# Rotating mixer A's queries before their norm, with the norm's factor in the softmax

## The chip, the cores and the metric

One core of a Trainium2 chip runs the whole kernel. The metric is the time of one execution on the device in microseconds (us), the median over several runs. The engines are TensorE (PE in the profile, with PEld for its weight loads), VectorE (DVE), ScalarE (ACT), GpSimd (POOL) and SyncE (SP, which issues most transfers).

## The reference, cut to what matters

The layer normalises its input, projects it once (`w_in`), runs two mixers over head groups beside each other, gates their outputs, projects once more (`w_out`), normalises and adds the input. 16 meta tokens stand ahead of 512 real ones, so keys count 528 and the queries whose output is kept 512. Mixer A, which the change touches, has 8 query heads of 128 columns and 2 key/value heads:

```python
def rmsnorm(x, g):
    r = lax.rsqrt(jnp.mean(xf * xf, axis=-1, keepdims=True) + NORM_EPS)
    return (xf * r * g).astype(x.dtype)
def gqa_axial_mixer(qa, ka, va, q_g, k_g, ang_row, ang_col, pos):
    q = axial_rope(rmsnorm(heads_first(qa, A_HEADS, HEAD_DIM), q_g), ang_row, ang_col)
    k = axial_rope(rmsnorm(heads_first(ka, A_KV_HEADS, HEAD_DIM), k_g), ang_row, ang_col)
    ...
        s = jnp.einsum('bkgqd,bksd->bkgqs', qs[0], k).astype(jnp.float32) * scale
        p = jax.nn.softmax(s, axis=-1)
        return jnp.einsum('bkgqs,bksd->bkgqd', p.astype(v.dtype), v)
```

`r` is one number for a token and a head. `q_g` has one gain for each of the 128 columns. `axial_rope` rotates columns 0 to 31 with 32 to 63 by the row angle, and 64 to 95 with 96 to 127 by the column angle; the real tokens alone are rotated by nonzero angles.

## The kernel before, in words

All matrix products run on pairs of rounded numbers, a high part and a low part (`xh`, `xl`; `wh`, `wl`; `qh`, `qlA`), three matmuls for one product. Weights come from DRAM in pieces of 512 KB into `st` (three buffers); `wsplit` makes the high part on ScalarE (line 154) and the low part on VectorE (line 155).

**Order of work.** TensorE's order is written by the kernel itself. Class `Lanes` keeps a clock of estimated matmul time. A piece of attention work is a generator that issues some matmuls and yields a lag; `lanes.poll()`, called between the matmuls of a projection, resumes the generators that are due. So the transposes, scores and products of the heads are strewn into the projections, and each matmul is pinned behind the one before it. The other engines' orders come from a planner that walks through the whole program by its own estimates. When an engine is free it takes, among the instructions that are ready, the one with the earliest place in the program. `tc.high_priority(n)` moves that place forward by n positions, and a negative n moves it back. `wsplit` runs 60 positions late (`AHEAD`). Each engine then works through its queue strictly in that order.

**Mixer A.** `keys_A` makes the two key heads, normed and rotated, and is done when the queries begin. `queries_A(g)` projects four query heads at once (g is 0, then 1): four accumulators `pd`, one for each 128 tokens, each of 4 heads x 128 columns. ScalarE scales them by the token's input norm into `qn` (line 650). The generator `turn` then takes one of the four tiles at a time: `head_norm` (lines 570 to 580) squares each head on ScalarE with a row sum, makes the factor with `rstd` (two small GpSimd instructions, lines 239 and 241), and scales each head by factor and gain on VectorE (line 578); `rope` (lines 582 to 593) makes the swapped half products on VectorE into `t2` (lines 588 and 590), multiplies by the cosines on GpSimd (line 592) and adds on VectorE (line 593).

`attention_A`, one generator per head, transposes the four tiles of its head (line 66, `tr<-ident,qn`), splits the result into `qh` and `qlA`, and for each of four tiles of 128 queries: six score matmuls into `sc` (one buffer of two banks), the row maximum on VectorE (`mxA`, line 546), its scaling by -1/sqrt(128) on GpSimd (line 547), the exponential on ScalarE with row sums (line 550), the reciprocal, and the scaling of the probabilities on GpSimd (line 553). After two tiles `p_times_v` transposes the probabilities (`tr`, two buffers shared with all transposes and `pv`), splits them (`ph`, line 306; `pl`, line 309), multiplies by the values into `pv`, and VectorE multiplies that with the head's gate (`gA`, line 558).

Around this, TensorE projects: queries of group 0, gates 0 and 1 of mixer A, queries of group 1, gates 2 to 7, then the output projection. The heads of group 0 run beside the second of these and the third, those of group 1 beside the gates and the start of the output projection. The first head of group 1 (h = 4) begins its transposes only when `turn` of group 1 has issued all its work.

Of the kernel before, what the change touches and what calls it, by code (L numbers as in the profile page):

```python
# [10 lines left out]
F32 = mybir.dt.float32  # L11
# [6 lines left out]
P = 128  # L18
# [90 lines left out]
def kernel(ctx: ExitStack, tc: tile.TileContext, xT, xn, xm, w_s, w_t, w_q, w_o,  # L109
# [127 lines left out]
    def rstd(dst, ss, n, rows=P):  # L237

        nc.gpsimd.tensor_scalar(out=dst, in0=ss, scalar1=1.0 / n, scalar2=EPS,
                                op0=ALU.mult, op1=ALU.add)  # L240
        nc.gpsimd.tensor_tensor(out=dst, in0=dst, in1=mhalf[:rows, :dst.shape[1]], op=ALU.pow)  # L241
# [188 lines left out]
    def two(t):  # L430
        return t.rearrange("p (a b) -> p a b", a=2)
# [86 lines left out]
    def attention_A(h, qn, q_task, k, k_task, v, v_task):  # L518
        while h == 4 and not q_task[3]:
            yield 0.3  # L520
        gs = lambda half: gA[h][:, half * 256:(half + 1) * 256]
        qh = ap.tile([P, SEQ], F32R, name="qh", tag="q1")
        ql = ap.tile([P, SEQ], F32R, name="qlA", tag="q2")
        tr = ptr.tile([P, 512], F32, name="tr", tag="tr")
        for t in range(TT):
            transpose(tr[:, t * P:(t + 1) * P], qn[t][:, h % 4, :], ident)
        hi(qh, tr)
        lo(ql, tr, qh)
        yield LAG["qA"]
        while not k_task[3]:  # L530
            yield 0.3
        kh, kl = k
        last = None
        for half in range(2):
            pts = []
            for t in (2 * half, 2 * half + 1):
                tq = slice(t * P, (t + 1) * P)
                mx = ap.tile([P, 1], F32, name="mxA", tag="mx", bufs=4)
                sm = ap.tile([P, 1], F32, name="smA", tag="sm", bufs=4)
                yield from room(1)  # L540
                sc = psc.tile([P, 2, 512], F32, name="sc", tag="sc")
                for i, (n0, n1) in enumerate(KEYS):
                    mm(sc[:, i, :HALF], qh[:, tq], kh[:, n0:n1], start=True, stop=False)
                    mm(sc[:, i, :HALF], qh[:, tq], kl[:, n0:n1], start=False, stop=False)
                    mm(sc[:, i, :HALF], ql[:, tq], kh[:, n0:n1], start=False, stop=True)
                nc.vector.tensor_reduce(out=mx, in_=sc[:, :, :HALF], op=ALU.max, axis=AX.XY)
                nc.gpsimd.tensor_scalar(out=mx, in0=mx, scalar1=-ASCALE, scalar2=1.0,
                                        op0=ALU.mult, op1=ALU.mult)
                p = ap.tile([P, NT], F32, name="p", tag="p", bufs=6)
                nc.scalar.activation(two(p), sc[:, :, :HALF], AF.Exp, scale=ASCALE, bias=mx,  # L550
                                     accum_out=sm)
                nc.vector.reciprocal(out=sm, in_=sm)
                nc.gpsimd.tensor_scalar(out=p, in0=p, scalar1=sm, scalar2=1.0,
                                        op0=ALU.mult, op1=ALU.mult)
                pts.append(p)
                if t % 2 == 0:
                    yield LAG["scA"]
            last = spawn_pv(v_task, p_times_v(pts, v, lambda pv, half=half: nc.vector.tensor_tensor(  # L558
                out=gs(half), in0=pv, in1=gs(half), op=ALU.mult), h), LAG["pA"])
            if half == 0:  # L560
                yield LAG["scA"]
        over[NH + h] = lanes.spawn(spill_A(h), 0.0, last)
# [7 lines left out]
    def head_norm(raw, n, g, rows=P):  # L570

        ss = ap.tile([P, 4], F32, name="ssh", tag="ssh", bufs=4)
        for i in range(n):
            jk = ap.tile([P, P], F32, name="jk", tag="jk")
            nc.scalar.activation(jk[:rows], raw[:, i, :], AF.Square, accum_out=ss[:rows, i:i + 1])
        rstd(ss[:rows, :n], ss[:rows, :n], P, rows)
        for i in range(n):
            nc.vector.scalar_tensor_tensor(out=raw[:, i, :], in0=raw[:, i, :],  # L578
                                           scalar=ss[:rows, i:i + 1], in1=g[:rows], op0=ALU.mult,
                                           op1=ALU.mult)  # L580

    def rope(x, cos, sin):

        t2f = ap.tile([P, NT], F32, name="t2", tag="tT")
        t2 = t2f[:, :4 * P].rearrange("p (n a r) -> p n a r", n=4, a=2)
        xv = x.rearrange("p n (a r) -> p n a r", a=2)
        sv = sin.rearrange("p n (a r) -> p n a r", a=2)
        nc.vector.tensor_tensor(out=t2[:, :, :, 0:32], in0=xv[:, :, :, 32:64],
                                in1=sv[:, :, :, 0:32], op=ALU.mult)
        nc.vector.tensor_tensor(out=t2[:, :, :, 32:64], in0=xv[:, :, :, 0:32],  # L590
                                in1=sv[:, :, :, 32:64], op=ALU.mult)
        nc.gpsimd.tensor_tensor(out=x, in0=x, in1=cos, op=ALU.mult)  # L592
        nc.vector.tensor_tensor(out=x, in0=x, in1=t2f[:, :4 * P].rearrange(
            "p (n d) -> p n d", n=4), op=ALU.add)

    def keys_A(pss):
# [33 lines left out]

        return (kh, kl), lanes.spawn(turn(), LAG["vals"])

    def queries_A(g):

        pss = [pd.tile([P, 512], F32, name="pd", tag="pd") for _ in range(TT)]
        for k0 in range(0, KT, 2):
            wh, wl = fetch()
            for k in (k0, k0 + 1):
                c = slice((k - k0) * 512, (k - k0 + 1) * 512)
                for t in range(TT):  # L640
                    ts_ = slice(NM + t * P, NM + (t + 1) * P)
                    mm(pss[t], xh[k][:, ts_], wh[:, c], start=(k == 0), stop=False)
                    mm(pss[t], xl[k][:, ts_], wh[:, c], start=False, stop=False)
                    mm(pss[t], xh[k][:, ts_], wl[:, c], start=False, stop=(k == KT - 1))
                    lanes.poll()
        res = []
        for t in range(TT):
            tag = "ql" if g == 0 else "fr" if t < 2 else "f"
            qn = ap.tile([P, 4, P], F32, name="qn", tag=tag, bufs=2 if tag == "fr" else 4)
            nc.scalar.activation(qn.rearrange("p n d -> p (n d)"), pss[t], AF.Copy,  # L650
                                 scale=rt[:, t:t + 1])
            res.append(qn)

        def turn():
            for t, qn in enumerate(res):
                head_norm(qn, 4, gqB)
                rope(qn, cosT[:, t:t + 1, :].broadcast_to([P, 4, P]),
                     sinT[:, t:t + 1, :].broadcast_to([P, 4, P]))
                yield LAG["norm"]

        return res, lanes.spawn(turn(), 0.0)


    for h in range(NH):
# [374 lines left out]
```

## Time and profile before

| what | value |
|---|---|
| median of 3 runs | 955.04 us (954.67 to 955.67) |
| the profiled execution, its own time | 955.66 us |
| its span in the profile | 953.9 us |
| TensorE busy | 926.4 us, 97% of the span |
| VectorE busy | 584.6 us, 61% |
| ScalarE busy | 482.0 us, 51% |
| GpSimd busy | 164.0 us, 17% |
| mean granted TensorE clock | 0.99 of full speed |

The span is what the profiler saw of one execution, from its first to its last event; the execution's own time is a little longer. Times inside the profile count from the start of the span. The busy time of TensorE counts matmuls from start to modelled end, so that back-to-back matmuls show as 100%. An arrow in a row (`<-`) says what ended the idle time ahead of an instruction.

### The profile page before, as it was taken

The numbers are of one execution on the slowest core, as the hardware profiler recorded it, in microseconds if no ns is written. First come the engines' busy times: TensorE is split into PE (matmuls) and PEld (weight loads), VectorE is DVE, ScalarE is ACT, GpSimd is POOL, SyncE is SP. The second block draws the span as 40 slices with busy tenths as digits, with TensorE's granted clock in tenths as the row PEclk, the third lists the DMA queues.
The fourth block names the chain that finished last, engine by engine and source line by source line (L and its number), as shares of the span: only waits on it lengthen the run. The fifth ranks groups of instructions, "written<-read, shape, count | busy, mean of one in ns | idle before, by whom it ended". The sixth has DMA issues, their size and how long they took to land.

```text
span 953.9 us, 14190 instructions
## 1 busy us (share of the span) xinstructions
PE 926.4 (97%) x5498; PEld 810.8 (85%) x5498; DVE 584.6 (61%) x974; ACT 482.0 (51%) x845; POOL 164.0 (17%) x250
## 2 busy tenths in 40 slices
PE   9999999999999999999999999998999999999983
PEld 8899898989989898998997888886888888888862
DVE  6386576757575574757554274447554662476996
ACT  6664655546464554746552254354555743245531
POOL 0001010101001010101201041226212123201054
PEclk9999999999999999999999999999999999999996
DMA  9742122222223222312223223211222346976785
GB/s 333 260 159 99 67 88 88 79 77 100 76 78 99 82 84 77 100 67 78 89 67 100 89 68 109 67 58 54 80 75 78 128 141 202 292 226 193 232 278 196
DMA packets 40611, 117.16 MB, mean 123 GB/s; under 512 B 4672, under 2 KB 9536, under 8 KB 40416
## 3 DMA queue, kind: packets, MB, share of 16 engines
q1 hardware_dynamic: 37072, 104.71, 33.2%
q0 software_dynamic: 3328, 11.54, 4.1%
q8 instruction: 43, 0.70, 0.3%
q14 instruction: 24, 0.20, 0.1%
q10 hardware_dynamic: 144, 0.01, 0.0%
HBM read 107.85 MB, written 8.39 MB: 122 GB/s over the span
## 4 chain that ended last, share of the span: by engine, by line
PE 84%; DVE 7%; DMA 2%; POOL 2%; ACT 2%; issue 1%; SPq 0%; DVEq 0%; POOLq 0%; ACTq 0%
PE pd L63 54%; PE po L63 14%; PE sc L63 6%; PE pv L63 5%; PE tr L66 5%; DVE wl L155 1%; DVE qn L578 1%; DMA st<-in_w_o_dram 1%; DVE y L939 1%; POOL qn L592 1%; DMA ch<-in_w_o_dram 1%; POOL ssh L241 1%; DMA xns<-in_xn_dram 1%; DMA xs<-in_xT_dram 1%; ACT qn L650 0%
## 5 line engine op out<-in xcount | busy, mean ns | idle before, releaser
L63 PE MATMUL pd<-xh,wh 128*128 128x264 f32 (+1 forms) x992 | 333.3, 336 | 0.0
L63 PE MATMUL pd<-xl,wh 128*128 128x264 f32 (+1 forms) x992 | 324.9, 327 | 0.4 <-DVE xl L180 0.4
L63 PE MATMUL pd<-xh,wl 128*128 128x264 f32 (+1 forms) x992 | 324.9, 328 | 0.4 <-DVE wl L155 0.4
L154 ACT ACTIVATE wh<-st 128x1024 fp32r<-128x1024 f32 (+2 forms) x135 | 139.8, 1038 | 208.3 <-PE pd L63 90.5
L155 DVE TENSOR_TENSOR wl<-st,wh 128x1024 fp32r<-128x1024 f32 (+2 forms) x135 | 161.7, 1198 | 98.9 <-ACT wh L154 97.7
L63 PEld LDWEIGHTS pd<-xh,wl 128*128 128x128 f32 x992 | 186.6, 188 | 17.8 <-DVE wl L155 0.7
L63 PEld LDWEIGHTS pd<-xh,wh 128*128 128x128 f32 x992 | 187.3, 189 | 12.9 <-ACT xh L179 0.2
L63 PEld LDWEIGHTS pd<-xl,wh 128*128 128x128 f32 x992 | 187.5, 189 | 12.0 <-DVE xl L180 0.6
L63 PE MATMUL po<-wh,ol 128*128 128x512 f32 x176 | 69.6, 396 | 0.9 <-DVE ol L309 0.9
L63 PE MATMUL po<-wh,oh 128*128 128x512 f32 x176 | 70.3, 400 | 0.0
L63 PE MATMUL po<-wl,oh 128*128 128x512 f32 x176 | 69.8, 397 | 0.0
L463 ACT ACTIVATE p<-p,mx 128x528 f32<-128x528 f32 x64 | 46.5, 728 | 34.2 <-POOL mx L460 34.0
L453 DVE CUSTOM_DVE_ANT_0 p<-sc,dist 128x528 f32<-128x528 f32 x64 | 44.9, 702 | 24.0 <-PE sc L63 23.5
L309 DVE TENSOR_TENSOR pl<-tr,ph 128x512 fp32r<-128x512 f32 x64 | 43.4, 688 | 16.2 <-ACT ph L306 15.0
L306 ACT ACTIVATE ph<-tr 128x512 fp32r<-128x512 f32 x64 | 37.6, 590 | 30.9 <-PE tr L66 30.6
L63 PE MATMUL pd<-wh,xh 128*128 128x512 f32 x128 | 52.2, 408 | 0.8 <-DVE vf L300 0.8
L66 PE MATMUL tr<-ident,p 128*128 128x128 f32 (+1 forms) x320 | 50.9, 273 | 1.7 <-DVE gA L558 0.9
L63 PE MATMUL pd<-wh,xl 128*128 128x512 f32 x128 | 50.6, 395 | 0.0
L63 PE MATMUL pd<-wl,xh 128*128 128x512 f32 x128 | 50.5, 395 | 0.0
L66 PEld LDWEIGHTS tr<-ident,p 128*128 128x128 f32 (+1 forms) x320 | 37.3, 132 | 13.4 <-DVE gA L558 1.6
L413 POOL TENSOR_SCALAR pm<-pm 32x256 fp32r<-32x256 f32 x32 | 20.1, 627 | 149.7 <-ACT pm L306 145.8
L460 POOL TENSOR_SCALAR mx<-mx 128x2 f32<-128x2 f32 x32 | 12.1, 377 | 196.0 <-DVE mx L453 196.0
(206 smaller groups left out, 1582.6 us busy)
## 6 DMA issues: line engine op xcount, KB each, us to landing
st<-in_w_t_dram SPq DMA_DIRECT2D x82, 512.0 KB, 3.6
st<-in_w_o_dram SPq DMA_DIRECT2D x40, 512.0 KB, 4.3
st<-in_w_q_dram SPq DMA_DIRECT2D x16, 512.0 KB, 3.6
xs<-in_xT_dram SPq DMA_DIRECT2D x16, 264.0 KB, 5.7
xns<-in_xn_dram SPq DMA_DIRECT2D x8, 512.0 KB, 5.3
ch<-in_w_o_dram POOLq DMA_DIRECT2D x8, 512.0 KB, 8.8
out_dram<-y SPq DMA_DIRECT2D x16, 256.0 KB, 2.3
os<-oscr SPq DMA_DIRECT2D x6, 512.0 KB, 3.6
```

The costliest lines, as they stand in the source:

```text
L63: self._add(self.nc.tensor.matmul(out, lhsT, rhs, start=start, stop=stop), us)
L66: self._add(self.nc.tensor.transpose(out, in_, ident), 0.109)
L154: nc.scalar.activation(wh[:, c], st[:, c], AF.Copy)
L155: nc.vector.tensor_tensor(out=wl[:, c], in0=st[:, c], in1=wh[:, c].bitcast(F32), op=ALU.subtract)
L241: nc.gpsimd.tensor_tensor(out=dst, in0=dst, in1=mhalf[:rows, :dst.shape[1]], op=ALU.pow)
L306: nc.scalar.activation(dst, src, AF.Copy)
L309: nc.vector.tensor_tensor(out=dst, in0=src, in1=h.bitcast(F32), op=ALU.subtract)
L413: nc.gpsimd.tensor_scalar(out=pm[32:64], in0=pm[0:32].bitcast(F32), scalar1=1.0, scalar2=1.0, op0=ALU.mult, op1=ALU.mult)
L453: nc.vector.tensor_tensor_reduce(out=two(p), in0=sc[:, :, :HALF], in1=two(dist[:, w0:w0 + NT]), scale=1.0, scalar=-3.0e38, op0=ALU.add, op ...
L460: nc.gpsimd.tensor_scalar(out=mx, in0=mx, scalar1=-0.125, scalar2=1.0, op0=ALU.mult, op1=ALU.mult)
L463: nc.scalar.activation(p2[m], p2[m], AF.Exp, scale=0.125, bias=mx[:, m:m + 1], accum_out=sm[:, m:m + 1])
L578: nc.vector.scalar_tensor_tensor(out=raw[:, i, :], in0=raw[:, i, :], scalar=ss[:rows, i:i + 1], in1=g[:rows], op0=ALU.mult, op1=ALU.mult)
```

## The change

`queries_A` no longer norms its queries. Each tile is squared in one ScalarE instruction into scratch `sqA` (tag `tT`, two buffers, which the rotation's scratch uses too), VectorE sums the squares by head into `ss`, the raw queries are rotated, and `ss` is turned into the factor times 1/sqrt(128) by `rstd` and one more GpSimd instruction. The factor enters in `attention_A`: it multiplies the row maximum (line 547) and is the scale of the exponential (line 550), a column of 128 numbers where there was a constant. The gain of 128 columns goes into the tables of cosines and sines once, in the new `gain_tables`, after the keys' rotations, which still use the bare tables. For the second group everything that `turn` issues stands 150 positions later in the planner's order; for the first group its place is unmoved.

```diff
--- before.py
+++ after.py
@@ -518,6 +518,7 @@
     def attention_A(h, qn, q_task, k, k_task, v, v_task):
         while h == 4 and not q_task[3]:
             yield 0.3
+        qn, ss = qn
         gs = lambda half: gA[h][:, half * 256:(half + 1) * 256]
         qh = ap.tile([P, SEQ], F32R, name="qh", tag="q1")
         ql = ap.tile([P, SEQ], F32R, name="qlA", tag="q2")
@@ -544,10 +545,11 @@
                     mm(sc[:, i, :HALF], qh[:, tq], kl[:, n0:n1], start=False, stop=False)
                     mm(sc[:, i, :HALF], ql[:, tq], kh[:, n0:n1], start=False, stop=True)
                 nc.vector.tensor_reduce(out=mx, in_=sc[:, :, :HALF], op=ALU.max, axis=AX.XY)
-                nc.gpsimd.tensor_scalar(out=mx, in0=mx, scalar1=-ASCALE, scalar2=1.0,
+                r = ss[:, t, h % 4:h % 4 + 1]
+                nc.gpsimd.tensor_scalar(out=mx, in0=mx, scalar1=r, scalar2=-1.0,
                                         op0=ALU.mult, op1=ALU.mult)
                 p = ap.tile([P, NT], F32, name="p", tag="p", bufs=6)
-                nc.scalar.activation(two(p), sc[:, :, :HALF], AF.Exp, scale=ASCALE, bias=mx,
+                nc.scalar.activation(two(p), sc[:, :, :HALF], AF.Exp, scale=r, bias=mx,
                                      accum_out=sm)
                 nc.vector.reciprocal(out=sm, in_=sm)
                 nc.gpsimd.tensor_scalar(out=p, in0=p, scalar1=sm, scalar2=1.0,
@@ -630,6 +632,19 @@
 
         return (kh, kl), lanes.spawn(turn(), LAG["vals"])
 
+    def gain_tables():
+
+        for i in range(2):
+            lanes.finish(kA[i][1])
+        nc.gpsimd.tensor_tensor(out=cosT, in0=cosT,
+                                in1=gqB[:, None, :].broadcast_to([P, TT, P]), op=ALU.mult)
+        sv = sinT.rearrange("p n (a r) -> p n a r", a=2)
+        gv = gqB.rearrange("p (a r) -> p a r", a=2)
+        for d, o in ((0, 32), (32, 0)):
+            nc.gpsimd.tensor_tensor(
+                out=sv[:, :, :, d:d + 32], in0=sv[:, :, :, d:d + 32],
+                in1=gv[:, None, :, o:o + 32].broadcast_to([P, TT, 2, 32]), op=ALU.mult)
+
     def queries_A(g):
 
         pss = [pd.tile([P, 512], F32, name="pd", tag="pd") for _ in range(TT)]
@@ -643,6 +658,8 @@
                     mm(pss[t], xl[k][:, ts_], wh[:, c], start=False, stop=False)
                     mm(pss[t], xh[k][:, ts_], wl[:, c], start=False, stop=(k == KT - 1))
                     lanes.poll()
+        if g == 0:
+            gain_tables()
         res = []
         for t in range(TT):
             tag = "ql" if g == 0 else "fr" if t < 2 else "f"
@@ -651,14 +668,23 @@
                                  scale=rt[:, t:t + 1])
             res.append(qn)
 
+        ss = ap.tile([P, TT, 4], F32, name="ssq", tag="ssq")
+
         def turn():
             for t, qn in enumerate(res):
-                head_norm(qn, 4, gqB)
-                rope(qn, cosT[:, t:t + 1, :].broadcast_to([P, 4, P]),
-                     sinT[:, t:t + 1, :].broadcast_to([P, 4, P]))
+                with tc.high_priority(-150 if g else 0):
+                    sq = ap.tile([P, NT], F32, name="sqA", tag="tT")[:, :SEQ].rearrange(
+                        "p (n d) -> p n d", n=4)
+                    nc.scalar.activation(sq, qn, AF.Square)
+                    nc.vector.tensor_reduce(out=ss[:, t, :], in_=sq, op=ALU.add, axis=AX.X)
+                    rope(qn, cosT[:, t:t + 1, :].broadcast_to([P, 4, P]),
+                         sinT[:, t:t + 1, :].broadcast_to([P, 4, P]))
+                    rstd(ss[:, t, :], ss[:, t, :], P)
+                    nc.gpsimd.tensor_scalar(out=ss[:, t, :], in0=ss[:, t, :], scalar1=ASCALE,
+                                            scalar2=1.0, op0=ALU.mult, op1=ALU.mult)
                 yield LAG["norm"]
 
-        return res, lanes.spawn(turn(), 0.0)
+        return (res, ss), lanes.spawn(turn(), 0.0)
 
 
     for h in range(NH):
```

## Rows read from the trace of the kernel before

**Rows 1.** The page: busy time, share of the span, instructions of each engine.
```profile
PE 926.4 (97%) x5498; PEld 810.8 (85%) x5498; DVE 584.6 (61%) x974; ACT 482.0 (51%) x845; POOL 164.0 (17%) x250
```

**Rows 2.** Table by stretch: busy us (instructions) per engine, TensorE's granted clock, DMA.
```profile
551.00:576.00 25.00, 24.95 (x110) 19.97 (x109) 18.60 (x35) 13.62 (x44) 11.07 (x12) 1.00 0.26 80
...
640.00:648.00 8.00, 7.22 (x41) 5.58 (x39) 5.82 (x12) 5.75 (x27) 5.29 (x6) 1.00 0.26 95
648.00:652.00 4.00, 1.02 (x5) 0.97 (x5) 1.27 (x4) 1.81 (x7) 2.56 (x5) 0.88 0.02 6
652.00:654.00 2.00, 2.00 (x8) 1.47 (x7) 1.71 (x6) 0.04 (x1) 1.48 (x4) 0.50 0.00 0
...
655.00:675.00 20.00, 19.09 (x105) 15.94 (x104) 15.89 (x30) 9.91 (x16) 8.81 (x10) 1.00 0.17 55
...
900.00:953.90 53.90, 35.71 (x141) 27.06 (x139) 44.19 (x57) 16.01 (x25) 23.03 (x26) 0.85 0.69 245
```

**Rows 3.** TensorE's waits between 550 and 680: us in total, times, longest.
```profile
PE sc L63 <- ACT p L550: 3.0, 1, 3.0
PE tr L66 <- DVE gA L558: 0.9, 1, 0.9
PE tr L66 <- DVE pl L309: 0.8, 1, 0.8
PE sc L63 <- DVE qlA L309: 0.2, 1, 0.2
```

**Rows 4.** TensorE in order of time, 640 to 675: start us, us, instruction.
```profile
651.03 0.59 PE L63 MATMUL sc<-kh,qh 128*128 128x264 f32 x1 [2.98 <-ACT p L550]
...
654.55 0.39 PE L63 MATMUL pd<-xl,wh 128*128 128x512 f32 x1
...
658.50 0.28 PE L63 MATMUL sc<-kh,qh 128*128 128x264 f32 x1
...
659.92 0.39 PE L63 MATMUL pd<-xh,wh 128*128 128x512 f32 x1
...
673.32 0.60 PE L66 MATMUL tr<-ident,qn 128*128 128x128 f32 x4
```

**Rows 5.** GpSimd in order of time, 630 to 675.
```profile
644.29 2.19 POOL L592 TENSOR_TENSOR qn<-qn,cosT 128x512 f32<-128x512 f32 x1 [2.38 <-DVE t L590]
646.57 0.69 POOL L239 TENSOR_SCALAR ssh<-ssh 128x4 f32<-128x4 f32 x1
...
648.87 1.01 POOL L241 TENSOR_TENSOR ssh<-ssh,mhalf 128x4 f32<-128x4 f32 x1
649.96 0.19 POOL L547 TENSOR_SCALAR mxA<-mxA 128x1 f32<-128x1 f32 x1
```

**Rows 6.** VectorE in order of time, 630 to 675.
```profile
645.87 0.70 DVE L546 TENSOR_REDUCE mxA<-sc 128x1 f32<-128x528 f32 x1
...
668.29 0.69 DVE L593 TENSOR_TENSOR qn<-qn,t 128x512 f32<-128x512 f32 x1 [1.18 <-POOL qn L592]
```

**Rows 7.** Groups by line and shape, 634 to 675: busy us, mean ns | idle before.
```profile
L592 POOL TENSOR_TENSOR qn<-qn,cosT 128x512 f32<-128x512 f32 x4 | 7.9, 1981 | 4.8 <-DVE t L590 4.8
L578 DVE SCALAR_TENSOR_TENSOR qn<-qn,ssh,gqB 128x128 f32<-128x128 f32 x16 | 6.4, 440 | 2.9 <-POOL ssh L241 2.9
...
L575 ACT ACTIVATE jk<-qn 128x128 f32<-128x128 f32 x16 | 4.8, 307 | 0.0
...
L650 ACT ACTIVATE qn<-pd,rt 128x512 f32<-128x512 f32 x4 | 2.7, 677 | 2.0 <-PE pd L63 2.0
...
L306 ACT ACTIVATE ph<-tr 128x512 fp32r<-128x512 f32 x4 | 2.3, 591 | 0.0
```

**Rows 8.** GpSimd in order of time, ahead of the first group's norm.
```profile
554.49 0.19 POOL L239 TENSOR_SCALAR ssh<-ssh 128x4 f32<-128x4 f32 x1 [47.85 <-ACT jk L575]
```

**Rows 9.** ScalarE in order of time, 676 to 700.
```profile
678.09 0.70 ACT L550 ACTIVATE p<-sc,mxA 128x528 f32<-128x528 f32 x1 [2.23 <-POOL mxA L547]
```

**Rows 10.** TensorE in order of time, 676 to 700.
```profile
682.26 0.28 PE L63 MATMUL sc<-kh,qh 128*128 128x264 f32 x1
```

## The prediction, made blind

> **What bounds the kernel now.** I read the page first. TensorE is busy 926.4 us of a span of 953.9 [rows 1], so a change to mixer A's norms can pay only where TensorE stands still or runs slowly. The busy share of the other engines decides nothing by itself. The question is where TensorE loses time near the lines that the diff touches.
>
> The second view is the table by stretch around the second group's norm [rows 2]. TensorE is busy 7.22 of 8 us from 640 to 648, 1.02 of 4 us from 648 to 652, and 19.09 of 20 from 655 to 675. In the two microseconds after the long gap the granted clock is 0.50, which is the 1.2 GHz level, and it is back at 1.00 from 655 on. The last stretch, from 900 on, has TensorE busy 35.71 of 53.9 us. That is the end of the output projection, and the diff doesn't touch it.
>
> The third view says what TensorE waited for between 550 and 680, which takes in both groups' norms [rows 3]. There are four waits: 3.0 us for an exponential (line 550), 0.9 for the product with the gate (line 558), 0.8 for the low part of a transposed probability (line 309), and 0.2 for a query's low part. The first three, 4.7 us, lie in the second group's norm. Nothing there waits for the first group's norm, beside which TensorE is busy 24.95 of 25 us with gate projections [rows 2].
>
> The fourth view prices the slow clock [rows 4]. From 651.03 to 654.55, 3.52 us, TensorE did six score matmuls, three projection matmuls, two transposes and one more projection matmul. At full clock the same six and three took from 658.50 to 659.92, 1.42 us. Nine in 1.42 put the other three at some 0.45, together 1.87. The clock therefore cost 1.65 us, say 1.7, and TensorE's whole loss in this stretch is 4.7 + 1.7 = 6.4 us.
>
> The fifth view, GpSimd's order of work, names the cause of the long wait [rows 5]. VectorE's maximum for the running head was finished at 645.87 + 0.70 = 646.57 [rows 6], but GpSimd's scaling of it (line 547) started at 649.96. In those 3.4 us GpSimd worked through two pairs of the norm's small instructions (lines 239 and 241, from 646.57 to 649.88). ScalarE's exponential waits for line 547, and the next scores need the bank that the exponential reads. The queue is in order, so instructions that nobody needed for another 20 us stood in front of one that TensorE needed at 648.05. The 0.8 us wait is of the same kind on VectorE: the norm's scalings, two rotation products and a weight split were ahead of line 309. The 0.9 us wait is a rotation's addition (line 593) that held VectorE idle for 1.18 us until GpSimd's product was done [rows 6], with line 546 and line 558 behind it.
>
> **The change, part by part.** (1) The norm's factor leaves the path to the transposes. Per tile, four squares of 0.307 us on ScalarE and four scalings on VectorE of 0.44 mean in this stretch go [rows 7]. One square over 512 columns comes. The nearest row is line 306's plain 128x512 copy at 0.59, and line 546 stands for the new reduction at 0.70. For the second group's four tiles that is 4.8 to about 2.4 us on ScalarE and 6.4 to about 2.8 on VectorE. None of it is on TensorE's path by itself. It shortens what line 309 and line 546 queue behind, by some 0.9 us of VectorE a tile. GpSimd keeps both small instructions of lines 239 and 241 and gets a third, a scaling like line 547's 0.19 [rows 5], bounded above by line 239's 0.69: 0.8 to 2.8 us in all, behind the same rank.
>
> (2) The rank. The second group's squares, reductions, rotations and factors stand 150 positions later, so the planner prefers a ready step of a head. It still doesn't hold an engine idle for a step that isn't ready. So at worst one long instruction of the norm is in front of line 547, the rotation's product, which took 2.19 at 644.29 [rows 5]. Without the tile's four scalings (4 x 0.44 = 1.8) and its two rotation products ahead of it on VectorE, 2 us and more, the maximum would end near 644.6. Plus 2.2, plus 0.19, an exponential of 0.8 and hand-overs of 0.15 gives 647.9. TensorE, without the 0.8 us wait, would arrive at 647.25. That leaves 0 to 0.6 us of the 3.0; I take 0.6, since the product is long against the gaps. Of the 0.8 us I leave 0.1. Of the 0.9 I leave 0.4 (between 0 and 0.9), because VectorE will still queue additions behind GpSimd's products. The clock's 1.7 us go altogether: the gap of about 1 us before 670 lies in a stretch whose granted clock stayed at 1.00 [rows 2].
>
> (3) The gain goes into the rotation tables: three products on GpSimd, one of 128x512 and two of half that. With line 592's 1.98 mean [rows 7] as the upper bound for each they cost at most 6 us, with half for the small ones 4. They need only the keys' rotations done. GpSimd stood idle for 47.85 us ahead of the first group's norm [rows 8], so they cost nothing. If they ran behind the queries instead, they would lengthen a chain of some 16 us (four rotations, priced with the third rival) to at most 22, against 25 us of gate projections [rows 2].
>
> (4) The exponential's scale becomes a column instead of a constant, and so does line 547's factor. Line 650, which reads a column as scale, takes 0.677 for 128x512 from the accumulators, and line 306, which reads none, 0.591 [rows 7]: 0.09 more for each of 32 exponentials, 2.8 us of ScalarE. In an undisturbed step the exponential starts at 678.09 and is done at 678.79 [rows 9], while the next scores start at 682.26 [rows 10]: 3.4 us of cover, so I count 0. Without that cover it would cost 2.8. The Trainium skill (ScalarE: Activation LUTs, What ACT_TABLE_LOAD costs) states that each column operand adds about 93 ns to an activation, which speaks against this change; the trace's 0.087 agrees. By its figure an exposed sum would be 3.0 in place of 2.8, and a covered one stays 0.
>
> (5) No matmul, transfer or waiting point of the TensorE order is added or taken, so SP's queue keeps its order. From TensorE's side everything behind 673 simply starts earlier. Weights are fetched as buffers come free, so the transfers move with it.
>
> In the first group the wait of 0.2 goes too. The sum: 6.6 at stake (6.4 + 0.2), less 0.6, 0.1 and 0.4 left over, is a gain of 5.5 us. The profiled execution took 955.66 (span 953.9 and 1.76 around it), which would be 950.2. The median of the runs is 0.62 lower, 955.04, so I forecast **949.5**.
>
> **The rivals.** *Half of it.* The planner orders the queues by its own times, which can differ from the chip's, where GpSimd's products are long (1.98 mean [rows 7]). Two instructions of the norm may then still run ahead of line 547. That leaves a wait of 1.5 to 3 us in one place, perhaps with part of the clock's loss: a gain of 2 to 4.5, a time of 950.5 to 953.
>
> *No change.* Rank decides only between steps that are ready at once. If the norm's instructions become ready in GpSimd's gaps just before line 547 does, the same queue forms. For it: the two pairs ran back to back in a gap [rows 5]. Against it: VectorE's and ScalarE's share falls anyway. Time 953.2 to 955.5.
>
> *Slower: head 4's queries come too late.* In front of the second group's first transposes, at 673.32 [rows 4], the last rotation is done at 668.29 + 0.69 = 668.98 [rows 6], 4.3 us ahead. TensorE would now arrive near 667, so a norm that ended where it does today would already take back 2 us. The new rank pushes the rotations later, and the squares share two scratch buffers with the rotations' products. A tile's rotation by itself is at most 0.7 + 2.2 + 0.7 plus hand-overs, some 4 us, so four one after the other from 641.5 end near 658: room of 9 us. The gain is eaten when the last one ends past 673, which needs twice the bare duration. Ending near 676 it gives some 957.5, a second slow-clock stretch included. For it speaks the size of the rank; against it, that VectorE is busy only 15.9 of 20 us from 655 to 675 [rows 2], the norm included.
>
> *The exposed exponential* (part 4) would take 2.8 back: 952.3; it counts with the half gain. *The end of the kernel* (from 900 on), where TensorE idles 18 us, may be ordered otherwise by the planner, for better or worse by 1 to 1.5 us.
>
> **How the numbers follow.** The forecast case (a gain of 4.5 to 7.5) gets 0.48, the half gain 0.20, no change 0.17, slower 0.15 (0.12 for the late queries, 0.03 for the end). What a measurement can tell from no change is about 0.2%, 1.9 us. So faster is 0.68, same 0.17, slower 0.15. The likeliest case's own range is 947.5 to 950.5. Below, I go to the full 6.6 and 1 us from a better end, 947.4. Above, the range takes in the half gain, no change, and the mildest slower cases, to 956.0. Some 0.05 is left out below and 0.13 above.
>
> **What would show it.** In the profile after, the table of waits of TensorE in the stretch of the second group's norm should hold no wait above 1 us, and the granted clock there should be 1.00. GpSimd's scaling of the maximum should follow VectorE's maximum within one instruction. The three table products should stand between 507 and 554. The first transposes of head 4 should not wait for line 593's addition, and should come at about 667. TensorE's other waits should be the same, only earlier. I am wrong if those transposes wait for an addition by more than 2 us, if line 547 still queues behind lines 239 and 241, or if the stretch gains its 5 us and the last 54 us give them back.

## The result, and the profile after

The changed kernel takes 958.05 us (median of nine runs, 955.9 to 961.3), the kernel before 955.62 in the runs beside it (nine, 954.7 to 956.4). The ratio is 1.0031, with an interval of 1.0017 to 1.0045: slower by 0.3%, 2.4 us, where 949.5 was forecast. The profiled execution of the changed kernel is the shortest of its nine, 955.9 with a span of 954.1. It can show where time went within it, but not the whole of the 2.4 us; further profiles of the same kernel and of its parts supply the rest.

The busy line of the page after, to set against [rows 1]:

```profile
PE 925.8 (97%) x5498; PEld 810.0 (85%) x5498; DVE 578.4 (61%) x950; ACT 480.5 (50%) x789; POOL 172.2 (18%) x261
```

TensorE has the same 5498 matmuls and the same busy time. VectorE and ScalarE have less to do, GpSimd 8.2 us more.

The table by stretch of the kernel after, with the columns of [rows 2]:

```profile
506.00:509.00 3.00, 1.58 (x8) 0.96 (x6) 1.26 (x2) 1.06 (x1) 3.00 (x4) 1.00 0.53 168
...
640.00:648.00 8.00, 7.15 (x42) 5.62 (x41) 5.29 (x10) 4.71 (x9) 5.28 (x9) 1.00 0.09 36
648.00:652.00 4.00, 2.77 (x15) 1.96 (x14) 3.11 (x7) 2.48 (x5) 3.37 (x4) 1.00 0.40 131
652.00:654.00 2.00, 2.00 (x13) 1.58 (x12) 1.97 (x5) 0.65 (x2) 1.83 (x3) 1.00 0.00 0
...
655.00:675.00 20.00, 18.18 (x101) 15.17 (x100) 11.29 (x19) 10.15 (x17) 7.13 (x12) 1.00 0.20 63
```

The gap at 648 is smaller and the granted clock is 1.00 right behind it, as forecast. But from 655 to 675 TensorE is now busy 18.18 us and no longer 19.09, and there is a new place: from 506 to 509 GpSimd is busy all of 3.00 us and TensorE 1.58. The same three microseconds of the kernel before:

```profile
506.00:509.00 3.00, 2.22 (x10) 1.50 (x9) 2.34 (x4) 0.56 (x1) 0.63 (x1) 1.00 0.36 141
```

What TensorE waited for in the kernel after, from 620 to 700, against [rows 3]:

```profile
PE sc L63 <- ACT p L552: 1.8, 1, 1.8
PE sc L63 <- DVE qlA L309: 0.8, 1, 0.8
PE tr L66 <- DVE pl L309: 0.7, 1, 0.7
PE sc L63 <- ACT qh L306: 0.4, 1, 0.4
```

The wait for the exponential is 1.8 and not 3.0, and it stands one step of scores later (step 2 below). The 0.8 for line 309's low part of a probability is still 0.7, and 1.2 us of waits for a query's two parts are new. The 0.9 for the product with the gate is gone. The 0.2 of [rows 3] lies ahead of this stretch, near 601, and hasn't gone: two waits of 0.2 stand there now. And ahead of 550 the first of these lines, from the kernel after, stands where the second stood before:

```profile
PE pd L63 <- DVE vf L300: 1.8, 1, 1.8
```

```profile
PE pd L63 <- DVE vf L300: 0.8, 1, 0.8
```

Three rows of TensorE in the kernel after let one follow its lag. The matmul that waits for the values, the first transposes of head 4 (673.32 before, [rows 4]) and the start of the last matmuls:

```profile
509.33 0.50 PE L63 MATMUL pd<-wh,xh 128*128 128x512 f32 x1 [1.75 <-DVE vf L300]
...
673.04 0.60 PE L66 MATMUL tr<-ident,qn 128*128 128x128 f32 x4
...
940.98 0.39 PE L63 MATMUL po<-wl,vh 128*128 128x512 f32 x1
```

The first of them began at 507.75 before. So TensorE is 1.6 us late there (0.6 of it from earlier on), still 1.6 late at the first group's transposes (575.13 against 573.56), 0.3 us ahead at head 4, level when the output projection begins, 0.7 late from 772 on, and 0.3 late at the start of the last matmuls (940.65 before). From the first group's transposes to head 4's, TensorE gained 1.9 us; 5.3 had been forecast for the second group.

### The profile page after: what moved, and what is told of

The parts are those of the page before. It is cut to its first block, busy times and chain, and to the rows that moved or that the text cites. A ratio compares the mean times of both kernels' runs of the same rounds, so it can differ in the third digit from the quotient of the medians.

```text
span 954.1 us, 14127 instructions
## 1 busy us (share of the span) xinstructions
PE 925.8 (97%) x5498; PEld 810.0 (85%) x5498; DVE 578.4 (61%) x950; ACT 480.5 (50%) x789; POOL 172.2 (18%) x261
## 4 chain that ended last, share of the span: by engine, by line
PE 86%; DVE 5%; DMA 3%; POOL 2%; ACT 2%; issue 1%; SPq 0%; DVEq 0%; POOLq 0%; ACTq 0%
PE pd L63 57%; PE po L63 14%; PE sc L63 5%; PE pv L63 5%; PE tr L66 4%; DMA st<-in_w_o_dram 1%; DVE wl L155 1%; DVE y L965 1%; DMA st<-in_w_s_dram 1%; DMA xns<-in_xn_dram 1%; POOL qn L594 0%; DMA os<-oscr 0%; PE ss L63 0%; DVE mxA L547 0%; ACT wh L154 0%
## 5 line engine op out<-in xcount | busy, mean ns | idle before, releaser
L552 ACT ACTIVATE p<-sc,mxA,ssq 128x528 f32<-128x528 f32 x32 | 25.3, 791 | 44.7 <-POOL mxA L549 44.4
```

## The experiments

Two theories stood at the start. *Tables*: the three table products are not free, since they meet the second key head's rotation. *Queue*: the rank changes nothing, and GpSimd's queue still carries the norm in front of the maximum. The rival to both was that the late rank or the new scale column costs the time. Ratios are to the kernel before on the same chip; times are medians.

**The rank left out (e1).** The changed kernel with

```
-                with tc.high_priority(-150 if g else 0):
+                with tc.high_priority(0):
```

> The changed kernel with the second group's rank set to 0. Theory A (rank is inert; the time is lost because the heads' scaled maximum still queues behind the norm's small instructions and rotation products on GpSimd): the instruction order of every engine is the same as with the rank, so the same time as the changed kernel, 957 to 958.5 median with runs spread over 3 to 5 us, and waits of the scores for the exponential of 1.5 us or more in the second group's norm. Theory B (the rank pushes the norm's work into the heads' way or too late): at least 1 us less than the changed kernel. Theory C (the table products in front of the values' scaling) and theory D (columns as scale): same as the changed kernel.

Measured: 957.31, ratio 1.0011 (0.9996 to 1.0027). The interval meets that of the changed kernel, and no more could differ: on all five engines the traces show the instructions in the same order with rank 0 as with -150. The rank in the diff is inert.

**The tables later (e2).** The query gain is loaded a second time from memory, so that the products can't start early, and they are called in the middle of the first group's projection:

```
+        load(gqB, gq)
...
+            if g == 0 and k0 == 10:
+                gain_tables()
...
-        if g == 0:
-            gain_tables()
```

> The changed kernel with the gain read once more from DRAM amid the first group's query projection, so that the three table products run some 20 us later, when no values wait for VectorE. Theory C: the wait of the projection for the values' scaling near 509 falls from 1.8 to 0.8 us and the median by 1.0, to about 957. If C were all that the change loses, it would fall to 955.6 or below. Theories A, B, D: the wait may go, the median stays within 1 us of the changed kernel, and the runs are spread as widely.

Measured: 956.53, ratio 1.0010 (0.9992 to 1.0027). The wait for the values is 0.8 again, and GpSimd's share of the stretch falls from 3.00 to 1.29, as the row of e2's table by stretch shows:

```profile
506.00:509.00 3.00, 2.23 (x13) 1.57 (x12) 1.60 (x5) 1.06 (x1) 1.29 (x1) 1.00 0.60 175
```

So the products caused that wait. The median is 1.5 us under the changed kernel's, which the times alone don't settle, their intervals overlapping. It isn't below the kernel before either, so the tables are not all that the forecast missed.

**The maximum's scaling on VectorE, after (e3) and before (e4).** One word of line 549, or of line 547 of the kernel before:

```
-                nc.gpsimd.tensor_scalar(out=mx, in0=mx, ...
+                nc.vector.tensor_scalar(out=mx, in0=mx, ...
```

> The changed kernel with the scaling of the row maximum on VectorE instead of GpSimd, so that no head's step passes through GpSimd ahead of its exponential. Theory A: no wait of the scores for an exponential above 0.5 us in the second group's norm, and 3 to 5 us less than the changed kernel, 953 to 955, the runs within 2 us. Theories B, C, D: within 1 us of the changed kernel.

> The kernel before with that one edit. Theory A: the wait of 3.0 us and the 1.7 us of half clock behind it go; 4 to 5 us less than before, 950.5 to 952. If what delayed the exponential was not GpSimd's queue but VectorE's or ScalarE's: within 1 us of before.

Measured: e3 955.14, ratio 0.9993 (0.9977 to 1.0009); e4 956.39, ratio 1.0003 (0.9987 to 1.0018). TensorE's waits from 600 to 700 in e3:

```profile
PE sc L63 <- ACT p L552: 1.3, 1, 1.3
PE tr L66 <- DVE pl L309: 0.5, 1, 0.5
```

Taken off GpSimd's queue, the maximum leaves 1.8 us of waits; the kernel after has 3.7 even in the shorter stretch above. By the starts of the same matmuls, e3's TensorE is 2.8 us behind the kernel before at the first group's transposes and 2.6 ahead at head 4's: 5.4 us won, where 5.3 had been forecast for the second group. The expectation of no wait above 0.5 was missed all the same. The maximum that ended at 647.45 + 0.70 = 648.15 is scaled at 649.69 only, since VectorE's queue now has a rotation's addition in front of it, which itself waits for GpSimd:

```profile
649.08 0.69 DVE L595 TENSOR_TENSOR qn<-qn,t 128x512 f32<-128x512 f32 x1 [0.93 <-POOL qn L594]
649.69 0.21 DVE L549 TENSOR_SCALAR mxA<-mxA,ssq 128x1 f32<-128x1 f32 x1
```

And 2.2 us are lost again near 760, where a transpose waits 1.7 for line 309.

In e4 the long wait of [rows 3] is gone too (the longest for an exponential is 0.5, while that for the product with the gate grows to 1.5), so the queue theory holds for both kernels. Yet e4 is no faster, against its expectation of 4 to 5 us less. By the starts of the same matmuls in the two profiles, TensorE is 2.8 us ahead of the kernel before from 680 to 740 and 1.1 behind at 764. In between lie a wait and a stretch at half clock, from e4's TensorE in order of time and its table by stretch:

```profile
760.46 0.40 PE L66 MATMUL tr<-ident,p 128*32 128x128 f32 x2 [2.02 <-DVE pl L309]
```

```profile
762.00:764.00 2.00, 2.00 (x6) 1.59 (x5) 1.90 (x4) 1.87 (x4) 1.61 (x2) 0.50 0.55 219
```

VectorE in the same order shows why: the low parts of the loaded outputs `os`, which the output projection wants later, are ahead of the running head's low part `pl`.

```profile
755.40 2.87 DVE L309 TENSOR_TENSOR ol<-os,oh 128x512 fp32r<-128x512 f32 x4 [0.36 <-ACT oh L306]
...
758.51 1.29 DVE L309 TENSOR_TENSOR ol<-os,oh 128x512 fp32r<-128x512 f32 x2 [0.24 <-ACT oh L306]
759.72 0.69 DVE L309 TENSOR_TENSOR pl<-tr,ph 128x512 fp32r<-128x512 f32 x1
```

**The tables alone (e5).** The kernel before with the three products in the same place, multiplying by ones in place of the gain (the output is unchanged); every other instruction keeps its order:

```
+        nc.gpsimd.tensor_tensor(out=cosT, in0=cosT,
+                                in1=ones[:, None, :].broadcast_to([P, TT, P]), op=ALU.mult)
...
+        if g == 0:
+            gain_tables()
```

> The kernel before with the three table products added at the place that the change gives them, multiplying by ones, and nothing else; the order of every other engine is unchanged. Theory C (the products run beside the keys' rotation, lengthen its addition on VectorE and so hold up the values' scaling behind it): the wait near 508 grows from 0.8 to 1.8 us, the median by 1.0, and by 2 or more where the gap is followed by a stretch at half clock. If the products are covered, as the prediction had it: the wait stays at 0.8 and the median within 0.4 us of before.

Measured: 957.39, ratio 1.0015 (1.0003 to 1.0027), 2.1 us more by the medians. The wait for the values is 1.8, and behind it e5's table by stretch shows the slow clock:

```profile
509.00:511.00 2.00, 1.66 (x5) 1.37 (x6) 2.00 (x3) 0.00 (x0) 1.08 (x1) 0.75 0.00 0
511.00:513.00 2.00, 2.00 (x6) 1.52 (x6) 0.16 (x1) 0.00 (x0) 0.00 (x0) 0.50 0.36 66
```

In its profile TensorE is 3.1 us late from 512 on (0.6 of it from ahead of this place), 3.2 late from 740 to 772 and 4.2 late behind that: 0.9 more is lost where a transpose waits 0.8 us for the product with the gate (line 558), with VectorE's order unchanged.

**The changed kernel again (e6).** No edit; beside e5 on the same chip, for a second profile.

> The changed kernel once more, for a second profile of it and more timed runs beside the experiments. Theory A with C: 957 to 958 median, about 2 us over before; near 509 a wait of 1.8 us, near 659 another of about 1.8; where the execution is one of the longer ones, half clock behind one of them. If its loss was chance: the median within 0.5 us of before.

Measured: 958.07, ratio 1.0025 (1.0014 to 1.0037). Its profiled execution took 959.0, and two rows of its table by stretch say what the first profile, of 955.9, lacks:

```profile
511.00:513.00 2.00, 2.00 (x7) 1.49 (x6) 0.00 (x0) 0.00 (x0) 0.00 (x0) 0.50 0.83 236
...
661.00:663.00 2.00, 2.00 (x6) 1.60 (x5) 1.28 (x2) 0.00 (x0) 0.69 (x1) 0.50 0.00 0
```

The same two waits of 1.8 us are each followed by a stretch at half clock, the 1.2 GHz level. Between the matmul that waits for the values and 512, TensorE's lag behind the kernel before grows from 0.7 to 2.2 us through this.

**Both kernels mended (e7, e8).** e7 is the changed kernel with the later tables of e2, the maximum on VectorE, and the splits of `os` ranked behind the heads' steps; e8 is the kernel before with the last two.

```
+        with tc.high_priority(-120):
             for i in range(2):
                 hi(oh[j + i], st[:, i * SEQ:(i + 1) * SEQ])
                 lo(ol[j + i], st[:, i * SEQ:(i + 1) * SEQ], oh[j + i])
```

> The changed kernel with three edits: the tables made later as in the second experiment, the maximum scaled on VectorE as in the third, and the splits of the heads' outputs loaded for the output projection ranked 120 positions later, so that they don't stand ahead of the last heads' steps. Theory A (and that what the third experiment won near 659 was given back near 760, where the transposes waited for VectorE behind those splits): 3 to 5 us less than before, 950.5 to 952.5. If the gain is given back wherever the planner's order moves: 954 to 956.

> The kernel before with the maximum scaled on VectorE and the same splits ranked later, without the rest of the change. Theory A: as in the fourth experiment no long wait near 651, and now no 2.0 us wait near 760 with half clock behind it: 951 to 953. Otherwise as the fourth experiment, 956.

Measured: e7 949.92, ratio 0.9940 (0.9925 to 0.9956); e8 953.19, ratio 0.9974 (0.9962 to 0.9987). In e7 TensorE is busy 20.00 of the 20 us from 655 to 675. With the other two mends in both, then, the edit with its tables made later is worth 3.3 us (953.19 less 949.92). That e7 comes near the forecast of 949.5 is a coincidence of size: 2.1 us of it are mends that the kernel before takes as well (e8), and no part of the forecast.

**The scale column alone (e9).** The kernel before with a column that holds the constant, in the exponential and in the maximum's scaling (the planner moves some steps of ScalarE and GpSimd for it):

```
-                nc.scalar.activation(two(p), sc[:, :, :HALF], AF.Exp, scale=ASCALE, bias=mx,
+                nc.scalar.activation(two(p), sc[:, :, :HALF], AF.Exp, scale=col_s, bias=mx,
```

> The kernel before with a column of 1/sqrt(128) as the exponential's scale and as the factor of the row maximum, where constants stood, and nothing else of the change. The planner moves some of ScalarE's and GpSimd's steps with it. Theory D (the longer exponential lengthens every step of a head): 0.16 us for each of 32 steps, up to 5 us more than before, and new waits of the scores. The prediction and theory A: exponentials of 0.79 us and no new wait but by 0.2 us in the step that already waits; within 1 us of before.

Measured: 955.17, ratio 0.9996 (0.9979 to 1.0013). The run as a whole costs nothing that can be measured, but it doesn't isolate the column: with the moved order the 3.0 us wait of [rows 3] shrinks to 0.5, and one of 2.2 us with a stretch at half clock behind it appears at 662. The kernel after shows the column better. Two stretches of its profile, 575 to 641 and 673 to 750, hold 24 of its 32 exponentials, and in each of them TensorE's lag behind the kernel before moves by 0.2 us at most.

**The rank alone (e10).** The kernel before with its second group's norm and rotation inside the same rank:

```
+                with tc.high_priority(-150) if g else ExitStack():
                     head_norm(qn, 4, gqB)
```

> The kernel before with the second group's norm and rotation ranked 150 positions later, and nothing else of the change. The order of GpSimd's and ScalarE's instructions stays as before, VectorE's moves in a few places. Theory A (a rank decides only between instructions that are ready at once): the wait of about 3 us for the exponential near 651 stays, the time within 0.7 us of before. If the rank worked as the prediction had it: 3 to 5 us less.

Measured: 956.14, ratio 1.0002 (0.9989 to 1.0014). Nine places in VectorE's order change in the traces, none on GpSimd or ScalarE, and the wait of 3.0 us for the exponential stays as it was.

**One factor for the group (e11, e12).** In place of a trio of small GpSimd instructions per tile, one trio over all 16 columns behind the last rotation; e11 on the changed kernel, e12 on e7.

```
+                    if t == TT - 1:
+                        sf = ss.rearrange("p t n -> p (t n)")
+                        rstd(sf, sf, P)
```

> The changed kernel with the factors of all four tiles of a group made at once behind the last rotation, three small GpSimd instructions in place of twelve; the tables, the rank and the columns as in the change, and the order of the other engines all but unmoved. Theory A (those small instructions stand ahead of the heads' maximum on GpSimd): no wait near 659 above 0.6 us and no half clock behind it, 1 to 2.5 us less than the changed kernel, 955.5 to 957. Otherwise: as the changed kernel, 957.5 to 958.5.

> The seventh experiment's kernel with the factors made at once as in the eleventh. Theory A: with the maximum scaled on VectorE no head's step passes GpSimd ahead of its exponential, so GpSimd's small instructions no longer matter there: 949 to 950.5, within 1 us of the seventh experiment.

Measured: e11 956.61, ratio 1.0007 (0.9994 to 1.0020); e12 949.19, ratio 0.9932 (0.9917 to 0.9947), the shortest of all by the median, though its interval overlaps e7's, so that no difference is shown. e11's expectation was half missed: the time came, the vanished wait didn't. Its wait for the exponential is longer than the changed kernel's, 2.6 us. GpSimd in order of time shows what stands in front this time: the power over 16 columns takes 2.91 us where one over four takes 1.02, and the maximum, ready at 650.60 + 0.70 = 651.30 on VectorE, gets its scaling at 656.12.

```profile
650.60 0.70 DVE L547 TENSOR_REDUCE mxA<-sc 128x1 f32<-128x528 f32 x1
...
652.33 2.91 POOL L241 TENSOR_TENSOR ssq<-ssq,mhalf 128x16 f32<-128x16 f32 x1
...
656.12 0.27 POOL L549 TENSOR_SCALAR mxA<-mxA,ssq 128x1 f32<-128x1 f32 x1
```

So fewer instructions in the same queue don't take the wait away. With the scaling out of GpSimd's queue (e3, e7, e12) the longest wait for an exponential there is 1.3 us, and behind it the clock stays at full speed.

## Why the prediction was wrong, step by step

Two steps failed. From a gain of 5.5 us forecast to a loss of 2.4 is a miss of 7.9. The larger part is step 2, the gain that was to come in the second group: 5.3 forecast, 1.9 and 0.9 in the two profiles. Step 3, the tables counted at nothing, took what was left, with a smaller loss near 772 (step 5).

**Step 3, the tables counted at nothing, failed.** The prediction saw GpSimd's idle stretch of 47.85 us [rows 8] as cover. It asked when the stretch ends and not what stands at its edge. Each product needs only that the last instruction that reads its part of a bare table has run. Those readers are the steps of the second key head's rotation, so the first product was ready in the middle of that rotation, and there the planner put it. GpSimd in order of time, kernel after:

```profile
505.60 0.85 POOL L644 TENSOR_TENSOR sinT<-sinT,gqB 128x256 f32<-128x256 f32 x1 [1.93 <-DVE t L590]
506.42 1.28 POOL L594 TENSOR_TENSOR kn<-kn,cosT 128x512 f32<-128x512 f32 x1
507.67 0.71 POOL L644 TENSOR_TENSOR sinT<-sinT,gqB 128x256 f32<-128x256 f32 x1
508.35 1.73 POOL L639 TENSOR_TENSOR cosT<-cosT,gqB 128x512 f32<-128x512 f32 x1
```

and VectorE beside it:

```profile
507.74 1.20 DVE L595 TENSOR_TENSOR kn<-kn,t 128x512 f32<-128x512 f32 x1 [1.88 <-POOL kn L594]
508.86 0.76 DVE L300 TENSOR_TENSOR vf<-pd,rB 128x264 f32<-128x264 f32 x2
```

The same instructions of the kernel before, GpSimd and then VectorE:

```profile
505.34 1.29 POOL L592 TENSOR_TENSOR kn<-kn,cosT 128x512 f32<-128x512 f32 x1 [2.27 <-DVE t L590]
```

```profile
506.66 0.69 DVE L593 TENSOR_TENSOR kn<-kn,t 128x512 f32<-128x512 f32 x1 [1.40 <-POOL kn L592]
507.27 0.76 DVE L300 TENSOR_TENSOR vf<-pd,rB 128x264 f32<-128x264 f32 x2
```

Everything here runs 0.6 us later in the profile after, from work ahead of this place. Beyond that, a table product in front of the keys' product makes it 0.5 us late (506.42 against 505.34), and the addition behind it takes 1.20 and not 0.69 us, another 0.5, while it runs beside the next table products (it takes 1.19 in e5 and 0.69 in e2, without them). Together that is the 1.0 us by which the values' scaling and TensorE's wait grow. The Trainium skill (GPSIMD Engine Reference, Specifications) lists GpSimd's interfaces to SBUF, the on-chip memory, as shared with VectorE, with contention for a VectorE instruction that has two inputs there. The addition here has two, and its stretch agrees. In some executions the slow clock follows and adds about 1.5. The size is 1.0 in the first profile, 2.5 in e6's (1.0 of wait and 1.5 of slow clock), 2.5 in e5's, and 2.1 by e5's medians. e2 shows that moving the products takes the wait away, e5 that they alone bring it. The forecast's upper bound of 6 us of GpSimd work was even generous (they took 0.85, 0.71 and 1.73); the mistake was where it went. The sign that the prediction named, products between 507 and 554, would nearly have passed them: they stand from 505.6 to 510.1.

**Step 2, the rank, failed on the mechanism, and cost the most.** The forecast let the rank drive all but one long instruction of the norm from in front of the maximum. The rank moved nothing (e1), and in e10 it left GpSimd's order alone. The maximum that had waited 3.4 us does come through in the kernel after: it ends at 648.33 and is scaled at 648.43. TensorE's scores there wait 0.4 and 0.8 us for parts of a query instead of 3.0 for the exponential. But the next maximum, which the kernel before scaled 0.1 us after its end, now meets the queue. VectorE and GpSimd in order of time, kernel after, where that maximum (line 547) ended at 653.28 + 0.70 = 653.98:

```profile
647.64 0.69 DVE L547 TENSOR_REDUCE mxA<-sc 128x1 f32<-128x528 f32 x1
...
653.28 0.70 DVE L547 TENSOR_REDUCE mxA<-sc 128x1 f32<-128x528 f32 x1
```

```profile
648.43 0.36 POOL L549 TENSOR_SCALAR mxA<-mxA,ssq 128x1 f32<-128x1 f32 x1 [1.26 <-DVE mxA L547]
...
653.31 1.29 POOL L594 TENSOR_TENSOR qn<-qn,cosT 128x512 f32<-128x512 f32 x1
654.69 0.69 POOL L239 TENSOR_SCALAR ssq<-ssq 128x4 f32<-128x4 f32 x1
655.47 1.02 POOL L241 TENSOR_TENSOR ssq<-ssq,mhalf 128x4 f32<-128x4 f32 x1
656.57 0.85 POOL L683 TENSOR_SCALAR ssq<-ssq 128x4 f32<-128x4 f32 x1
657.50 0.40 POOL L413 TENSOR_SCALAR pm<-pm 32x256 fp32r<-32x256 f32 x1
658.00 0.26 POOL L549 TENSOR_SCALAR mxA<-mxA,ssq 128x1 f32<-128x1 f32 x1
```

These are the same lines 239 and 241 as in [rows 5], now with line 683 behind them, and this maximum waits 4.0 us for its scaling. TensorE stands 1.8 us for it, since its own other work covers more. That line 549 queues behind lines 239 and 241 is the prediction's own sign of being wrong (there the scaling is line 547, as in the kernel before). The prediction allowed one long instruction of the norm in front; here it is the product and three small ones.

The queue is that of the rival "no change", which had 0.17: a rank decides only between steps that are ready at once. But on the chip both were ready when GpSimd ended its product at 654.60, the sums that line 239 reads at 652.68 + 0.68 = 653.36, the maximum at 653.98, both on VectorE. So the planner's own times must have had them apart, which is what the rival "half of it" named (0.20), and one wait of 1.5 to 3 us with perhaps part of the clock's loss is what it priced. The planner's times stand in no trace, so this last step is inferred. That GpSimd's queue is what cost the gain is shown: with the maximum out of it e3 wins 5.4 us over the same stretch.

In the first profile TensorE wins 2.7 us by 655 (less waiting, and full clock behind it), loses 2.1 at the new wait, and wins 1.1 at 670, where the kernel before waits for the product with the gate. Of the 5.3 us forecast for the second group 1.9 came in that profile and 0.9 in e6's, where the half clock follows the new wait (TensorE's lag goes from 2.25 at the first group's transposes to 1.4 at head 4's). The clock's loss of 1.7 that the prediction priced is about right: in e4, which has no such wait, the same matmuls take 1.5 us less.

**Step 1, the norm's own work, was right in its sizes.** In the second group the four squares take 2.5 us and the four reductions 2.7 (forecast 2.4 and 2.8). The third small instruction of each tile comes to 1.7 us of GpSimd in all, within the 0.8 to 2.8 given, but not behind a rank: line 683's 0.85 is part of the queue above. So the cover named for it was false. Nor did the shorter VectorE work do what step 2 drew from it: the forecast left 0.1 of the 0.8 us wait for line 309, and 0.7 stayed, with a weight split still in front.

**Step 4, the column, was right.** The exponential takes 0.79 against 0.70, and TensorE's lag stands still beside 24 of the 32.

**Step 5 held in part.** No transfer got in the way, and the matmul lists are the same. But a smaller loss appears near 772, 0.7 us in the first profile and, with 0.3 of it already near 764, 1.3 in e6's. There a transpose waits for the product with the gate, where the kernel before has no wait:

```profile
772.29 0.66 PE L66 MATMUL tr<-ident,p 128*128 128x128 f32 x4 [0.58 <-DVE gA L560]
```

In VectorE's order a split of `os` now goes ahead of a head's maximum, at 759.37. That such splits can cost time is shown by e4 and, with them ranked behind, by e7 and e8, which lose nothing here. But whether that split is the cause in the changed kernel stays open, since e5 loses 0.9 in the same place with VectorE's order unchanged.

**The rivals on the slower side** did not occur. Head 4's queries were ready early: the last addition ran at 661.57, its transposes at 673.04 (667 had been forecast). The slower result came from a mechanism that was not among them, the tables, because step 3 had closed it. The sum, each term from the starts of the same matmuls against the profile of before: in the first profile +1.0 for the tables, -1.9 for the second group, +0.7 near 772, together -0.2, where that execution took 0.2 more than the profiled one of before (955.9 against 955.66); in e6's +2.5, -0.9 and +1.3, together +2.9, where it took 3.3 more (959.0). The sums leave out by how much an execution already differs ahead of 500 (0.6 late in the first profile, 0.3 early in e6's). The medians' +2.4 lies between them.

## What to carry to other kernels

Idle time of an engine is cover only for work that is sure to run inside it: ask when moved work becomes ready, and look at what that engine does for the path in the next two microseconds, since the planner here started it right there. A rank among ready steps doesn't keep an in-order queue free for a step that becomes ready a little later; take the urgent small instruction out of that queue (here one word, GpSimd to VectorE), see what stands in front of it in the new queue, and use a rank where the traces show that it moves the order, as with the splits of `os` (956.39 in e4, 953.19 in e8). When a wait near the path is mended, follow TensorE's lead to the end of the kernel: e4 was 2.8 us ahead at 740 and had lost them, and 1.1 more, at 764.

## What the runs showed of the hardware that was not expected

- A wait of TensorE of 1.8 us was followed by a granted clock of 0.50 in some executions (e5 and e6 at 511) and by 1.00 in another of the same kernel (the first profile of the kernel after, over the same stretch). The stretch at half clock cost 1.5 us. So one order of instructions gave 955.9 in one profiled execution and 959.0 in the next.
- GpSimd's 128x512 rotation products took 2.2 us where a weight split of VectorE (line 155, two inputs) had begun some 0.15 us before them, and 1.3 elsewhere, so that the mean of 1.98 [rows 7] mixes two kinds. All four products of the second group took 1.3 in the kernel after, where no split began so. Beside VectorE's scalings (line 578) the product took 1.3 in the kernel before too, and there the scalings were the longer: three took 2.37 us together, where four took 1.13 at 663.14 with no product beside them. In these pairs the instruction that began second was the one that took longer. GpSimd and then VectorE, kernel before:

```profile
656.58 1.33 POOL L592 TENSOR_TENSOR qn<-qn,cosT 128x512 f32<-128x512 f32 x1
659.67 2.21 POOL L592 TENSOR_TENSOR qn<-qn,cosT 128x512 f32<-128x512 f32 x1 [1.77 <-DVE t L590]
```

```profile
655.95 2.37 DVE L578 SCALAR_TENSOR_TENSOR qn<-qn,ssh,gqB 128x128 f32<-128x128 f32 x3
...
659.52 1.21 DVE L155 TENSOR_TENSOR wl<-st,wh 128x1024 fp32r<-128x1024 f32 x1
```

- The power on GpSimd (line 241) took longer with more columns: 1.02 us for four, 2.91 for sixteen (e11).
